# Which of three waits the last VectorE instruction carries itself

## The chip, the cores and the metric

One core of a Trainium2 chip. The metric is the device time of one execution in microseconds. Every run gives several; medians are quoted with the range. A profiled execution's span runs from its first to its last instruction and is some 1.4 us shorter than its time.

## The reference

The input `x` is 32 x 512 rows of 1024 floats, 67.1 MB. The output is the mean of `max(x, 0)` over each row.

```python
relu_x = np.maximum(x, 0)
return np.mean(relu_x, axis=-1).astype(np.float32)
```

## The kernel before

Each of 128 partitions holds 128 rows. Blocks of 16 rows are loaded into three buffers; ScalarE (ACT) sums the even rows, VectorE (DVE) the odd ones. The last row of each partition is cut into three loads so that little is left to do when the last bytes arrive. ScalarE sums columns 0-447, VectorE 448-575 and 576-767, each into a spare column behind the row. The last VectorE instruction sums columns 768-1023 and the three spare columns in one pass, scaled by 1/1024. It needs three things: the third load, VectorE's own two partial sums, and ScalarE's.

```python
    col_pieces = [576, 192, 256]
    # ... (loads, all issued by SyncE; loaded[k] counts to 16 when load k is complete)
    nc.scalar.wait_ge(loaded[i + 1], 16)
    act_row(nc, last[:, :448], last[:, D:D + 1]).then_inc(act, 1)
    nc.vector.wait_ge(loaded[i + 1], 16)
    dve_row(nc, last[:, 448:576], last[:, D + 1:D + 2])
    nc.vector.wait_ge(loaded[i + 2], 16)
    dve_row(nc, last[:, 576:768], last[:, D + 2:D + 3]).then_inc(dve, 1)
    nc.vector.wait_ge(dve, n_done + 1)          # VectorE's own sums
    nc.vector.wait_ge(loaded[i + 3], 16)        # the third load
    nc.vector.wait_ge(act, n_done + 1)          # ScalarE's sum
    nc.vector.scalar_tensor_tensor(
        out=last[:, 768:], in0=last[:, 768:], scalar=0.0, in1=scale[:, :], op0=ALU.max, op1=ALU.mult,
        accum_out=res[:, J - 1:J],
    ).then_inc(dve, 1)
    # ... SyncE waits for dve and stores the results
```

In the built program an engine's instruction carries one wait. Of several written in a row, the one written first is carried; the others go into a separate instruction (EVENT_SEMAPHORE) ahead of it, in reversed order. Here the separate instruction holds ScalarE's sum first and the load second, and the last instruction carries VectorE's own sum.

Of the kernel before, what the change touches and what calls it, by code (L numbers as in the profile page):

```python
# [17 lines left out]
def dve_row(nc, src, acc, init=None):  # L18

    return nc.vector.tensor_scalar(  # L20
        out=src, in0=src, scalar1=0.0, scalar2=init,
        op0=ALU.max, op1=ALU.add, accum_out=acc,
    )
# [22 lines left out]
def kernel(  # L46
# [10 lines left out]
    nc = tc.nc  # L57
# [36 lines left out]
    act, dve, pool = (nc.alloc_semaphore(n) for n in ("act", "dve", "pool"))  # L94
# [78 lines left out]
    for n in row_pieces[:-1]:  # L173
# [10 lines left out]
    n_done = i + 1  # L184
# [8 lines left out]
    dve_row(nc, last[:, 448:576], last[:, D + 1:D + 2])  # L193
    nc.vector.wait_ge(loaded[i + 2], 16)
    dve_row(nc, last[:, 576:768], last[:, D + 2:D + 3]).then_inc(dve, 1)
    nc.vector.wait_ge(dve, n_done + 1)
    nc.vector.wait_ge(loaded[i + 3], 16)
    nc.vector.wait_ge(act, n_done + 1)  # L198
    nc.vector.scalar_tensor_tensor(  # L199
        out=last[:, 768:], in0=last[:, 768:], scalar=0.0, in1=scale[:, :], op0=ALU.max, op1=ALU.mult,  # L200
        accum_out=res[:, J - 1:J],
# [51 lines left out]
```

## Time and profile before

| | before |
|---|---|
| time, 3 runs | 161.41 us (161.35 to 161.50) |
| span of the profiled execution | 159.8 us |

The page, the chain and the timeline of this stretch, and the moments at which the three conditions came true, are shown within the prediction; ScalarE's sum is the last of the three. Such a moment is the increment of a semaphore. It is read from the trace's records, to the nanosecond; no view of the profile prints it.

### The profile page before, as it was taken

The page shows a single profiled execution, that of the slowest core. Times are in us where ns is not written, and L with a number is a line of the kernel's source. Part 1 is how long each engine was busy: PE and PEld are TensorE (multiplying, and loading weights), DVE is VectorE, ACT ScalarE, POOL GpSimd, SP SyncE. Part 2 cuts the span into 40 slices and gives each one's busy share as a digit, 9 for nine tenths or more (in the row PEclk, how much of TensorE's full clock was granted, in tenths as well). Part 3 has the DMA queues.
Part 4 walks back from the last instruction along what each step waited for, and adds up shares of the span by engine and source line. Part 5 has one row for each costly group of instructions (what it writes and reads, how often), then busy time and mean ns, then how long its engine had stood idle before and what let it go on. Part 6 is the DMA issues. An engine that isn't in the chain of part 4 may idle for free.

```text
span 159.8 us, 350 instructions
## 1 busy us (share of the span) xinstructions
DVE 73.5 (46%) x133; ACT 70.4 (44%) x133; POOL 1.3 (1%) x9
## 2 busy tenths in 40 slices
DVE  0000029900498005970079500894009920199975
ACT  1400029800497005950079300892009900199974
POOL 1000000000000000000000000000000000000001
DMA  9969979999799699699699699799997997999993
GB/s 394 492 295 525 459 328 525 394 394 525 344 443 525 279 509 525 262 525 525 262 525 509 279 525 459 328 525 394 394 525 344 443 525 344 410 423 393 418 411 110
DMA packets 2456, 67.18 MB, mean 420 GB/s; under 512 B 536, under 2 KB 792, under 8 KB 1176
## 3 DMA queue, kind: packets, MB, share of 16 engines
q1 hardware_dynamic: 2456, 67.18, 97.9%
HBM read 67.11 MB, written 0.07 MB: 420 GB/s over the span
## 4 chain that ended last, share of the span: by engine, by line
DMA 84%; DVE 12%; SPq 1%; issue 1%; ACT 0%; DVEq 0%
DMA rows<-in_x_dram 56%; DMA last<-in_x_dram 29%; DVE rows L20 12%; SPq L109 1%; ACT last L15 0%; DVE last L199 0%; DVEq L198 0%; SPq L115 0%
## 5 line engine op out<-in xcount | busy, mean ns | idle before, releaser
L20 DVE TENSOR_SCALAR_CACHE_REDUCE rows<-rows 128x1024 f32<-128x1024 f32 (+1 forms) x63 | 72.1, 1208 | 78.8 <-DMA rows<-in_x_dram 78.7
L15 ACT ACTIVATE rows<-rows 128x1024 f32<-128x1024 f32 x64 | 66.3, 1038 | 84.0 <-DMA rows<-in_x_dram 83.7
L15 ACT ACTIVATION_READ_ACCUMULATOR rows<-rows 128x1 f32 x64 | 12.1, 189 | 0.0
L20 DVE DVE_READ_ACCUMULATOR rows<-rows 128x1 f32 x63 | 5.2, 83 | 0.0
L168 DVE STREAM_TRANSPOSE turned<-mean 128x32 f32<-128x32 f32 x1 | 0.2, 211 | 5.8 <-ACT row L164 5.8
L164 ACT ACT_TABLE_LOAD x1 | 1.3, 1283 | 3.2 <-DMA row<-in_x_dram 3.2
L157 POOL TENSOR_SCALAR res<-sums 128x112 f32<-128x112 f32 (+1 forms) x2 | 0.5, 250 | 153.8 <-DVE rows L20 153.8
L164 ACT ACTIVATE row<-row 128x1024 f32<-128x1024 f32 x1 | 1.1, 1057 | 0.0
L20 DVE TENSOR_SCALAR_CACHE_REDUCE last<-last 128x128 f32<-128x128 f32 (+1 forms) x2 | 0.6, 320 | 0.0
L15 ACT ACTIVATE last<-last 128x448 f32<-128x448 f32 x1 | 0.6, 577 | 0.1
L199 DVE SCALAR_TENSOR_TENSOR last<-last,scale 128x259 f32<-128x259 f32 x1 | 0.4, 429 | 0.2 <-ACT last L15 0.2
L142 POOL MEMSET scale<- 128x259 f32 x1 | 0.3, 315 | 0.0
L187 POOL TENSOR_SCALAR res<-part 128x1 f32<-128x1 f32 x1 | 0.3, 267 | 0.6 <-DVE rows L20 0.6
L15 ACT ACTIVATION_READ_ACCUMULATOR last<-last 128x1 f32 x1 | 0.2, 188 | 0.0
L164 ACT ACTIVATION_READ_ACCUMULATOR row<-row 128x1 f32 x1 | 0.2, 187 | 0.0
L20 DVE DVE_READ_ACCUMULATOR last<-last 128x1 f32 x2 | 0.2, 83 | 0.0
L141 POOL MEMSET mean<- 128x32 f32 x1 | 0.1, 125 | 1.5 <-POOLq L55 1.5
L237 POOL MEMSET const-bfloat16-1.0<- 128x1 bf16 x1 | 0.1, 102 | 0.0
L237 POOL MEMSET const-uint8-127<- 128x1 uint8 x1 | 0.1, 102 | 0.0
L237 POOL MEMSET const-float32-0.0<- 128x1 f32 x1 | 0.1, 99 | 0.2 <-issue 0.2
L237 POOL MEMSET const-float32-1.0<- 128x1 f32 x1 | 0.1, 99 | 0.0
L199 DVE DVE_READ_ACCUMULATOR last<-last,scale 128x1 f32 x1 | 0.1, 84 | 0.0
## 6 DMA issues: line engine op xcount, KB each, us to landing
rows<-in_x_dram SPq DMA_DIRECT2D x1, 3584.0 KB, 38.0
rows<-in_x_dram SPq DMA_DIRECT2D x1, 2048.0 KB, 42.5
rows<-in_x_dram SPq DMA_DIRECT2D x1, 1024.0 KB, 44.5
row<-in_x_dram SPq DMA_DIRECT2D x1, 512.0 KB, 3.2
rows<-in_x_dram SPq DMA_DIRECT2D x1, 512.0 KB, 45.3
last<-in_x_dram SPq DMA_DIRECT2D x1, 288.0 KB, 45.6
last<-in_x_dram SPq DMA_DIRECT2D x1, 128.0 KB, 45.2
rows<-in_x_dram SPq DMA_DIRECT2D x7, 48.7
```

The source lines that it names most:

```text
L15: return nc.scalar.activation(out=src, in_=src, func=ACT.Relu, accum_out=acc)
L20: return nc.vector.tensor_scalar(out=src, in0=src, scalar1=0.0, scalar2=init, op0=ALU.max, op1=ALU.add, accum_out=acc,)
L109: nc.sync.dma_start(out=dst, in_=src).then_inc(loaded[i], 16)
L141: nc.gpsimd.memset(mean0[:, :], 0.0)
L142: nc.gpsimd.memset(scale[:, :], inv).then_inc(pool, 1)
L157: nc.gpsimd.tensor_scalar(out=res[:, lo:hi], in0=sums[:, lo:hi], scalar1=inv, scalar2=0.0, op0=ALU.mult, op1=ALU.add,).then_inc(pool, 1)
L164: nc.scalar.activation(out=row0[:, :], in_=row0[:, :], func=ACT.Relu, scale=inv, accum_out=mean0[:, 0:1],).then_inc(first, 1)
L168: nc.vector.transpose(turned0[:, :], mean0[:, :]).then_inc(first, 1)
L187: nc.gpsimd.tensor_scalar(out=res[:, J - 2:J - 1], in0=part[:, 0:1], scalar1=part[:, 1:2], scalar2=inv, op0=ALU.add, op1=ALU.mult,).then_i ...
L199: nc.vector.scalar_tensor_tensor(out=last[:, 768:], in0=last[:, 768:], scalar=0.0, in1=scale[:, :], op0=ALU.max, op1=ALU.mult, accum_out=r ...
L237: nc = _bacc.Bacc("TRN2", target_bir_lowering=False, num_devices=1)
```

## The change

The order in which three waits are written. The intent: the instruction that is held for the last bytes should wait for them itself, and not through a separate instruction in front of it.

```diff
-    nc.vector.wait_ge(dve, n_done + 1)
     nc.vector.wait_ge(loaded[i + 3], 16)
     nc.vector.wait_ge(act, n_done + 1)
+    nc.vector.wait_ge(dve, n_done + 1)
     nc.vector.scalar_tensor_tensor(
```

In the built program the separate instruction now holds VectorE's own sum first and ScalarE's second, and the last instruction carries the load.

## The prediction

> **What bounds the kernel now.** I read the page from the top. The copies are the work: 67.11 MB are read at a mean of 420 GB/s in a span of 159.8 us, while VectorE and ScalarE are busy for less than half of it. The page's first two parts and its chain say so:
>
> ```profile
> span 159.8 us, 350 instructions
> DVE 73.5 (46%) x133; ACT 70.4 (44%) x133; POOL 1.3 (1%) x9
> ...
> HBM read 67.11 MB, written 0.07 MB: 420 GB/s over the span
> ...
> DMA 84%; DVE 12%; SPq 1%; issue 1%; ACT 0%; DVEq 0%
> ```
>
> What to see: the last entry, VectorE's sequencer (DVEq), has a share that rounds to nothing. The change touches that entry alone, so everything before the last few hundred nanoseconds can be left out. Next I read the end of the chain in order of time (start, length, what, in us):
>
> ```profile
> 111.47 45.58 DMA last<-in_x_dram
> 157.05 0.02 issue
> 157.07 0.06 ACT last L15
> 157.13 0.42 issue
> 157.55 0.20 ACT last L15
> 157.75 0.03 issue
> 157.78 0.05 DVEq L198
> 157.83 0.04 issue
> 157.87 0.12 DVE last L199
> ```
>
> This is the list that decides the case. The last row comes in three loads (columns 0-575, 576-767, 768-1023). The chain leaves the first of them at 157.05, runs through ScalarE's sum of columns 0-447, and reaches the last VectorE instruction through a waiting instruction of 0.05 us. It does not pass through the third load, the one this change is about. The timeline of the same stretch shows the VectorE side and the store (start, length, engine, line, operation, and in brackets the idle time before it):
>
> ```profile
> 157.07 0.58 ACT L15 ACTIVATE last<-last 128x448 f32<-128x448 f32 x1
> 157.34 0.35 DVE L20 TENSOR_SCALAR_CACHE_REDUCE last<-last 128x192 f32<-128x192 f32 x1
> 157.55 0.19 ACT L15 ACTIVATION_READ_ACCUMULATOR last<-last 128x1 f32 x1
> 157.62 0.08 DVE L20 DVE_READ_ACCUMULATOR last<-last 128x1 f32 x1
> 157.87 0.43 DVE L199 SCALAR_TENSOR_TENSOR last<-last,scale 128x259 f32<-128x259 f32 x1 [0.17 <-ACT last L15]
> 158.34 0.34 SPq L210 DMA_DIRECT2D out_dram<-res  x1
> ```
>
> The last VectorE instruction waits for three things, and the order in which they came true is the whole question. From the trace's record of semaphore increments, to the nanosecond: the third load's sixteenth increment is at 157.645, VectorE's own partial sum at 157.711, ScalarE's partial sum at 157.749. The load is first by 0.104 us and ScalarE is last, which is what the bracket above names.
>
> **What the Trainium skill says.** (1) "Perfetto Trace Analysis", section "DVE / Act Engine Instruction (TENSOR_ADD, Activation, etc)": such an instruction is pushed into a wait queue, its semaphores are met there, and it then moves on to the engine, while the sequencer is free for the next one. So a wait carried by the instruction should end in a start with little between. The trace agrees: the first load of the last row counts full at 157.047, and both engines start on it at 157.070 and 157.071, 0.023 to 0.024 us later. (2) The same page, "Identifying Dependency Chains": an instruction that waits for several engines may get EventSemaphore instructions ahead of it for the additional conditions. The trace shows one, on line 198, from 157.776 to 157.826, and the engine's instruction starts at 157.871. A condition met there thus costs 157.871 - 157.749 = 0.122 us from increment to start, against 0.024 us for a carried one: 0.098 us more. That difference is what moving a wait between the two places can be worth. (3) "VectorE: DVE Perf Modes", section "The DRAIN you can't avoid": a result read by the next instruction of the same engine is not safe without a semaphore between. The last instruction reads VectorE's two partial sums, so its wait on its own engine has to stay somewhere; the change keeps it, in the other place. No trace here tests that danger.
>
> **The change part by part.** In the built programs both kernels have the same instructions in the same order on every engine. The three waits are distributed differently. Before: the separate instruction holds (ScalarE's sum, third load), and the last VectorE instruction carries the wait for VectorE's own sum. After: the separate instruction holds (VectorE's own sum, ScalarE's sum), and the last VectorE instruction carries the third load. So:
>
> - Added: nothing. Removed: no instruction and no wait. The separate instruction still has two conditions, so I keep its 0.050 us.
> - Before, the separate instruction ends its wait at max(157.749, 157.645) = 157.749. After, at max(157.711, 157.749) = 157.749. Difference 0.000 us.
> - The carried wait is for 157.711 before and 157.645 after. Both precede the end of the separate instruction, 157.826, by over 0.11 us, so neither holds anything. Difference 0.000 us.
> - Behind it everything is as before: 0.43 us for the instruction, then the store of 7.5 KB. SyncE is released 157.871 + 0.465 = 158.336, and its last wait ends at 159.795, 1.46 us later. (4) The skill's "DMA: Bandwidth & Descriptors", section on where the fixed cost of about 2 us goes, puts most of that cost into the receipt of the written data; 1.46 us here for a tiny transfer fits in kind, and the change does not touch it.
> - The loads are all issued by 112.881 by SyncE, and no later issue waits on anything moved here, so the copies are untouched.
>
> Sum in the profiled execution: 0.000 us. The removal of the load from the separate instruction pays only in executions in which the load is the last of the three. With a lateness d beyond ScalarE's sum, before starts at load + 0.122, after at the later of load + 0.024 and ScalarE's sum + 0.122; so the gain is the smaller of d and 0.098 us. For d to be above zero the third load has to land more than 0.702 us after the first (157.749 - 157.047), against 0.598 us in the profile. The two loads between them are 96 KB + 128 KB, so their rate would have to fall by some 15%. I estimate that perhaps one execution in six does that, with a gain of some 0.05 us each: 0.01 us on the mean. That frequency is my choice; a single profile cannot give it.
>
> **The rivals.** *The load is often last without the profiler.* The intent of the change suggests that its author saw it so. For it: the slack is only 0.104 us, and the profiled execution (161.16 us) was 0.25 us shorter than the median of the others (161.41), so the copies may well fall differently. Against it: both the load and ScalarE's work start from the same stream, so a delay of all of it moves both. If every execution were so, the gain is at most 0.098 us: 161.31 us, still within 0.1%. *The order of the two conditions inside the separate instruction matters.* Its 0.050 us are against 0.021 us for VectorE's other separate waits, which hold one condition. If they are checked one after the other at some 0.029 us each, before pays the second check after ScalarE's sum has arrived, while after has the first check behind it by then: up to 0.029 us gained, 161.38 us. Against it: the record starts only at 157.776, 0.027 us after ScalarE's increment, so it may be a fixed execution time that comes after both conditions. I give this one chance in three. *The change takes something away.* With the load carried, a late load and a late sum could add up if the queue checked the load only after the separate instruction and needed longer for a load's semaphore than for the engine's own. Nothing in the profile speaks for that: 0.024 us is what carried loads show. It would make at most a few hundredths, 161.45 us. *ScalarE's sum stops being the last*, so that VectorE's own sum, at 157.711, binds: not possible by this change, which moves no work.
>
> **Range and chances.** 161.41 less 0.01 for the late loads and 0.01 (0.029 by one third) for the order of the checks makes 161.39 us. All mechanisms together span 161.28 (both gains in full) to 161.45. The three runs before lie within 0.15 us of each other, and a new set of runs may sit a tenth or two off for reasons of the copies alone, since the 67 MB are 84% of the chain and 0.1% of their rate is 0.13 us. I take 161.2 to 161.62. Two per cent would be 3.2 us, over thirty times the largest effect that I can build, so nearly all the chance is on "within 2%".
>
> **What would show it right or wrong.** In the profile of the changed kernel: equal instruction counts; the separate instruction, now on the line of the VectorE wait, still about 0.05 us long and still released by ScalarE's accumulator read; the last VectorE instruction some 0.12 us after ScalarE's increment, with the idle time before it near 0.17 us. If that distance is nearer 0.09 us, the order of the checks matters. If the load's last increment comes after ScalarE's, the instruction should start 0.024 us behind the load, and the first rival holds. I would be wrong if the time moved by over 0.3 us with the end of the trace unchanged, for then the copies moved, or if the separate instruction became longer or split in two.

## The result, and the profile after

The changed kernel took 161.16 us (median of 6 runs, 161.07 to 161.67) against 161.41 us (161.15 to 161.62, 6 runs): ratio 0.9990, 95% interval 0.9974 to 1.0006. A ratio is the mean time of one kernel's fast runs over that of the other's of the same rounds, so it is not quite the ratio of the medians. No difference is clear of noise.

The page of the changed kernel answers the first one line by line:

```profile
span 160.0 us, 350 instructions
DVE 73.5 (46%) x133; ACT 70.3 (44%) x133; POOL 1.3 (1%) x9
...
HBM read 67.11 MB, written 0.07 MB: 420 GB/s over the span
...
DMA 84%; DVE 12%; SPq 1%; issue 1%; ACT 0%; DVEq 0%
```

Same counts, same rate, same chain. This one execution has a span 0.2 us longer, because its copies came later: the first load of the last row is complete at 157.29 us instead of 157.05. So times from the span's start must not be compared across the two; distances from that load may be. The chain in order of time (start, length, what):

```profile
157.29 0.02 issue
157.31 0.06 ACT last L15
157.37 0.42 issue
157.79 0.20 ACT last L15
157.99 0.04 DVEq L198
158.03 0.04 issue
158.08 0.12 DVE last L199
```

Between ScalarE's accumulator read and the separate instruction (DVEq) stood a piece "issue" (time in which the engine waited for nothing that the profile shows) of 0.03 us; it is gone. From the first load to the last VectorE instruction it is 0.788 us here and 0.824 us before, so the end comes 0.036 us sooner. The timeline shows the idle time before the last instruction, which was marked 0.17 us; it is no longer marked, because it fell to 0.134 us and the timeline leaves out idle time under 0.15:

```profile
157.58 0.35 DVE L20 TENSOR_SCALAR_CACHE_REDUCE last<-last 128x192 f32<-128x192 f32 x1
157.79 0.19 ACT L15 ACTIVATION_READ_ACCUMULATOR last<-last 128x1 f32 x1
157.86 0.08 DVE L20 DVE_READ_ACCUMULATOR last<-last 128x1 f32 x1
158.08 0.43 DVE L199 SCALAR_TENSOR_TENSOR last<-last,scale 128x259 f32<-128x259 f32 x1
```

The semaphore records say why. VectorE's own sum is counted at 157.955, the separate instruction starts at 157.983, and ScalarE's sum is counted at 157.990. The separate instruction has started before its second condition is met. In the kernel before, it started 0.027 us behind ScalarE's increment; here, 0.028 us behind VectorE's own. The profile's start of such an instruction follows its first condition. The load (157.878) was early again and held nothing.

### The profile page after: what moved, and what is told of

It is laid out like the page before. It is cut to its first block, busy times and chain, and to the rows that moved or that the text cites. A ratio compares the mean times of both kernels' runs of the same rounds, so it can differ in the third digit from the quotient of the medians.

```text
span 160.0 us, 350 instructions
## 1 busy us (share of the span) xinstructions
DVE 73.5 (46%) x133; ACT 70.3 (44%) x133; POOL 1.3 (1%) x9
## 4 chain that ended last, share of the span: by engine, by line
DMA 84%; DVE 12%; SPq 1%; issue 1%; ACT 0%; DVEq 0%
DMA rows<-in_x_dram 56%; DMA last<-in_x_dram 29%; DVE rows L20 12%; SPq L109 1%; ACT last L15 0%; DVE last L199 0%; DVEq L198 0%; SPq L115 0%
## 5 line engine op out<-in xcount | busy, mean ns | idle before, releaser
L15 ACT ACTIVATE rows<-rows 128x1024 f32<-128x1024 f32 x64 | 66.2, 1036 | 84.0 <-DMA rows<-in_x_dram 83.8
```

The costliest lines, as they stand in the source:

```text
L15: return nc.scalar.activation(out=src, in_=src, func=ACT.Relu, accum_out=acc)
```

## The experiments

Two theories at the outset. **S (serial)**: the separate instruction checks its conditions one after the other, so the place of a wait in it matters. **R (removal)**: what matters is that the load left the separate instruction. For the 0.25 us in the medians there are two more: **C**, that the change affects the copies, and **N**, that it is noise. Distances are between semaphore increments and starts, from the traces. All twelve runs gave correct results. Four variants ran only once (161.09, 161.29, 161.25 and 162.03 us, in the order of this section); only distances within their traces are read.

### The changed kernel once more

No edit.

> The changed kernel once more, timed in five rounds, because the first comparison left 0.25 us (161.16 against 161.41), seven times the 0.034 us that the ends of the two traces differ by. Theory S (the separate instruction checks its two conditions one after the other; the profile's start of it is the moment when the first is met): the last VectorE instruction starts at the later of first condition + 0.122 us and second condition + at most 0.088 us, so here about 0.088 us behind ScalarE's increment, and the time is 0.03 us below before: ratio 0.9998. Rival C (the copies became faster by the change): ratio again near 0.9985.

161.16 us (161.07 to 161.47) against 161.42 us; ratio 0.9988, 0.9974 to 1.0003. In this profile the load is the last of the three: it is counted 0.728 us behind the first load, ScalarE's sum 0.700, VectorE's own 0.663. The last instruction starts at 0.785, which is VectorE's own + 0.122 and ScalarE's + 0.085. So even with the load last, the load held nothing: a carried wait would have let the instruction start at some 0.751. C and N stay open.

### The order within the separate instruction

```diff
     nc.vector.wait_ge(loaded[i + 3], 16)
-    nc.vector.wait_ge(act, n_done + 1)
     nc.vector.wait_ge(dve, n_done + 1)
+    nc.vector.wait_ge(act, n_done + 1)
```

> The changed kernel with the two conditions of the separate instruction swapped: ScalarE's sum first, VectorE's own second; the load stays carried by the last instruction. Theory S: ScalarE's sum is now the first to be checked and the last to come, so the last instruction starts 0.122 us behind its increment, as in before. Rival R (what matters is that the load left the separate instruction): 0.088 us, as in the changed kernel.

The chain of this variant:

```profile
157.49 0.20 ACT last L15
157.69 0.03 issue
157.71 0.05 DVEq L198
157.76 0.04 issue
157.81 0.12 DVE last L199
```

The piece "issue" of 0.03 us ahead of the separate instruction is back, and the last instruction starts 0.122 us behind ScalarE's increment, as in the kernel before, although the load is carried. So R is wrong: taking the load out of the separate instruction gained nothing here, and the 0.036 us are due to the order.

### The load first in the kernel before

```diff
     nc.vector.wait_ge(dve, n_done + 1)
-    nc.vector.wait_ge(loaded[i + 3], 16)
     nc.vector.wait_ge(act, n_done + 1)
+    nc.vector.wait_ge(loaded[i + 3], 16)
```

> The kernel before with the two conditions of the separate instruction swapped: the load first, ScalarE's sum second; the instruction still carries the wait for VectorE's own sum. Theory S: at most 0.088 us from ScalarE's increment to the start, although the load is still in the separate instruction; the separate instruction's record starts 0.027 us behind the load's last increment, before ScalarE's. Rival R: 0.122 us, as in before.

This run missed its aim. In the profiled execution the load was the last by 0.170 us, so ScalarE's sum did not bind and the 0.088 us could not be seen:

```profile
157.86 0.03 issue
157.89 0.05 DVEq L198
157.94 0.04 issue
157.99 0.12 DVE last L199
```

What it does show: the separate instruction starts 0.028 us behind the load, now its first condition, and the last instruction 0.123 us behind it. The cost of the first place is the same for a load's semaphore as for an engine's.

### Carrying the wait that comes last

```diff
-    nc.vector.wait_ge(dve, n_done + 1)
-    nc.vector.wait_ge(loaded[i + 3], 16)
     nc.vector.wait_ge(act, n_done + 1)
+    nc.vector.wait_ge(dve, n_done + 1)
+    nc.vector.wait_ge(loaded[i + 3], 16)
```

> The last instruction carries the wait for ScalarE's sum, which comes last; the separate instruction holds the load first and VectorE's own sum second. Theory S: start at the latest of load + 0.122, own sum + at most 0.088, ScalarE's sum + 0.024: with the spacings of before (load 0.104, own sum 0.038 ahead of ScalarE's) at most 0.050 us behind ScalarE's increment, so some 0.07 us earlier than before; ratio about 0.9996, which five rounds may not resolve. Rival R: the load is in the separate instruction, so 0.122 us.

The chain goes straight from ScalarE to the last instruction, and the separate instruction (its own entry, durations in ns) is longer, since it starts at the load and waits inside for VectorE's own sum:

```profile
157.50 0.20 ACT last L15
157.69 0.04 issue
157.73 0.12 DVE last L199
```

```profile
L198 DVEq EVENT_SEMAPHORE  x1: 102/102/102, 157.6 to 157.6; - x1
```

The start is 0.041 us behind ScalarE's increment and 0.080 us behind VectorE's own, so VectorE's own sum, as the second condition, now sets it. From the first load it is 0.741 us: 0.083 less than in the kernel before, 0.047 less than in the changed one. The time was 161.33 us (161.02 to 161.47), ratio 0.9997, 0.9983 to 1.0011: a gain of this size isn't seen in the time. R is refuted once more, with the load in the separate instruction.

### The same with VectorE's own sum first

```diff
     nc.vector.wait_ge(act, n_done + 1)
-    nc.vector.wait_ge(dve, n_done + 1)
     nc.vector.wait_ge(loaded[i + 3], 16)
+    nc.vector.wait_ge(dve, n_done + 1)
```

> As the variant that carries ScalarE's sum, with the separate instruction's conditions swapped: VectorE's own sum first, the load second. Theory S: start 0.122 us behind VectorE's own increment, so about 0.085 us behind ScalarE's (own sum 0.038 us ahead in before), 0.035 us later than with the load first. If the order did not matter, as with the load first.

The start is 0.122 us behind VectorE's own increment and 0.086 us behind ScalarE's, 0.786 us from the first load: as S had it, 0.045 us later than with the load first.

### A load that comes last on purpose

All three of these have this edit (and a `scale` buffer of 643 columns in place of 259), with the waits of before, of the changed kernel, and with the load first in the separate instruction:

```diff
-    col_pieces = [576, 192, 256]
+    col_pieces = [320, 64, 640]
-    act_row(nc, last[:, :448], last[:, D:D + 1]).then_inc(act, 1)
+    act_row(nc, last[:, :192], last[:, D:D + 1]).then_inc(act, 1)
-    dve_row(nc, last[:, 448:576], ...); dve_row(nc, last[:, 576:768], ...); the rest: last[:, 768:]
+    dve_row(nc, last[:, 192:320], ...); dve_row(nc, last[:, 320:384], ...); the rest: last[:, 384:]
```

> The case that the change is meant for, made on purpose: the last row's loads are 320, 64 and 640 columns wide and ScalarE sums 192 of them, VectorE 128 and 64, so that the third load comes last by some 0.3 us (both partial sums some 0.5 us behind the first load, the third load 352 KB at 420 GB/s = 0.84 us behind it). Waits as in before: the separate instruction has ScalarE's sum, then the load; the instruction carries VectorE's own. Theory S: the load is the second condition, the first long met, so the last instruction starts at most 0.088 us behind the load's last increment, and the separate instruction's record is stretched: it starts 0.027 us behind ScalarE's increment. Without serial checks: 0.122 us behind the load.

> The same late load with the waits of the changed kernel: the instruction carries the load. Start 0.024 us behind the load's last increment, 0.06 us (theory S) to 0.10 us (no serial checks) sooner after the load than with the waits of before. The time falls by as much, under 0.1%, which three rounds may not resolve.

> The same late load, the separate instruction holding the load first and ScalarE's sum second. Theory S: the late one is the first condition, so 0.122 us behind the load's last increment, 0.034 us or more later than with the load second. If only the place of a wait counts and not its order: the same distance as with the load second.

The chains, with the waits of before (first the separate instruction's own entry), then of the changed kernel, then with the load first:

```profile
L198 DVEq EVENT_SEMAPHORE  x1: 389/389/389, 157.4 to 157.4; - x1
```

```profile
112.48 45.26 DMA last<-in_x_dram
157.74 0.04 DVEq L198
157.78 0.04 issue
157.82 0.12 DVE last L199
```

```profile
112.58 45.21 DMA last<-in_x_dram
157.79 0.02 issue
157.81 0.07 DVE last L199
```

```profile
112.49 45.59 DMA last<-in_x_dram
158.07 0.03 issue
158.10 0.05 DVEq L198
158.15 0.04 issue
158.20 0.12 DVE last L199
```

In the first the separate instruction is recorded as running for 389 ns: it starts 0.027 us behind ScalarE's increment and 0.354 us before the load's. From the load's last increment to the last instruction it is 0.079 us with the load second, 0.023 us with the load carried, and 0.122 us with the load first. All three sizes of S are thereby measured on the same, clearly last condition. (The 352 KB of the first expectation are the second and the third load together.) In the time, the first two are 161.51 and 161.50 us, with ratios to before of 1.0017 (0.9994 to 1.0040) and 1.0011 (0.9988 to 1.0034): 0.056 us between them can't be resolved. The third, a single run of 162.03 us, had its third load 1.338 us behind the first, against 0.957 and 0.923; its time is not compared.

### Is there more in the time than in the trace?

A null run of the kernel before against itself, and again the changed kernel and the variant that carries ScalarE's sum, on the same rounds; then the changed kernel a fourth time.

> The kernel before, unchanged, timed against itself: how far apart two identical kernels come out in five rounds. If by 0.1% (0.16 us), then the 0.0010 to 0.0012 by which the changed kernel lay below in two comparisons needs no cause in the change (theory N, noise of the copies). If within 0.0003, the 0.15 to 0.25 us wants a cause beyond the 0.034 us at the end of the trace (theory C).

> The changed kernel on the same rounds. Theory N: ratio anywhere from 0.9985 to 1.001, and about as far from 1 as the null run. Theory C: 0.9988 a third time, with the null run at 1.000. In its profile the last VectorE instruction starts 0.122 us behind VectorE's own increment, unless ScalarE's comes over 0.043 us later than that or the load over 0.099 us later.

> The variant that carries ScalarE's sum on the same rounds: its trace ended 0.04 us sooner than the changed kernel's after the first load of the last row. Theory N: ratio within 0.0015 of 1, its order against the changed kernel left to chance. In its profile the start is 0.080 us behind VectorE's own increment, or 0.122 us behind the load's if that is later than 0.042 us before VectorE's own.

> The changed kernel a fourth time against before. So far 0.9990, 0.9988 and 0.9993, each with 1 in its interval, and the null run at 1.0010; the ends of the traces give 0.9998 (0.037 us), or 0.9997 (at most 0.056 us) when the third load is late. Theory N: the fourth ratio lies anywhere between 0.9985 and 1.0010. Theory C (a part of the gain that the end of the trace doesn't show): again 0.9985 to 0.9995. In its profile, the start is the latest of own sum + 0.122, ScalarE's sum + 0.080 and load + 0.023.

| kernel, against before | median us | ratio | 95% interval |
|---|---|---|---|
| before itself | 161.35 against 161.19 | 1.0010 | 0.9991 to 1.0030 |
| changed | 161.14 against 161.19 | 0.9993 | 0.9978 to 1.0007 |
| carrying ScalarE's sum | 161.09 against 161.19 | 0.9993 | 0.9978 to 1.0008 |
| changed, fourth time | 161.15 against 161.17 | 0.9992 | 0.9976 to 1.0008 |

Two identical kernels came out 0.1% apart, as far as the changed one from before. Yet four ratios of the changed kernel, 0.9990, 0.9988, 0.9993 and 0.9992, all lie below 1. I therefore looked at all runs together, after the fact: 52 of the kernel before have a mean of 161.34 us, 24 of the changed one 161.20. Most of this 0.13 us comes from executions above 161.3 us, 23 of 52 and 4 of 24. The runs below it have means of 161.15 and 161.13 us, 0.02 apart, which is near what the trace shows. The variant that carries ScalarE's sum, with a shorter end than both, had 5 of 12 above 161.3 us. That speaks against a link between the waits and the slower executions, but the cut was chosen after the fact.

Taken as independent comparisons, the four ratios average 0.9991, give or take 0.0008 (an estimate from their intervals). That lies below 1, and just holds the 0.9998 that the ends of the traces lead to expect. So a gain beyond the traces is neither shown nor excluded. The profiles show where slower executions lose their time. In the two of the kernel before, timed at 161.16 and 161.19 us, the first load of the last row is complete at 157.05 and 157.08 us. In the four of the changed kernel, timed at 161.11, 161.23, 161.36 and 161.70 us, it is complete at 157.04, 157.08, 157.29 and 157.64 us. From there to the end of the timed execution it is 4.06 to 4.15 us in all six. So nearly all of the difference between executions arises in the copies, ahead of the waits that were changed, and the copies of the changed kernel are at most 0.004 us earlier than those of before. That is no sign of C, but six profiles do not decide it: C against N stays open.

## Why the prediction was right or wrong

All traces follow one formula. The last instruction starts at the latest of: first condition of the separate instruction + 0.122 us, second condition + 0.080 us, carried condition + 0.023 us. The first number was taken from the trace of before, the second from the first run that carries ScalarE's sum, the third from the late load with the waits of the changed kernel. In the other eleven profiles the first number sets the start in eight and the second in three; the third sets it in none of them, so it is measured once, for a load. (For ScalarE's sum, the second profile that carries it shows a start 0.028 us behind its increment, so the delay is no longer than that.) In ns from the last increment of the first load:

| profile (first, second; carried) | load | own | ScalarE | formula | measured |
|---|---|---|---|---|---|
| before (ScalarE, load; own) | 598 | 664 | 702 | 824 | 824 |
| before, null run (the same) | 554 | 646 | 700 | 822 | 823 |
| changed (own, ScalarE; load) | 588 | 665 | 700 | 787 | 788 |
| changed, second profile | 728 | 663 | 700 | 785 | 785 |
| changed, third | 727 | 659 | 700 | 781 | 782 |
| changed, fourth | 593 | 654 | 701 | 781 | 782 |
| (ScalarE, own; load) | 592 | 680 | 701 | 823 | 823 |
| (load, ScalarE; own) | 870 | 696 | 700 | 992 | 993 |
| (load, own; ScalarE) | 566 | 661 | 700 | 741 | 741 |
| (load, own; ScalarE), second | 554 | 649 | 701 | 729 | 729 |
| (own, load; ScalarE) | 585 | 664 | 700 | 786 | 786 |
| late load (ScalarE, load; own) | 957 | 671 | 576 | 1037 | 1036 |
| late load (own, ScalarE; load) | 923 | 680 | 583 | 946 | 946 |
| late load (load, ScalarE; own) | 1338 | 685 | 588 | 1460 | 1460 |

The records of the separate instruction show what the first two numbers are made of. It starts 0.027 to 0.029 us behind its first condition. It ends 0.050 us later (0.054 once), or 0.035 to 0.036 us behind its second condition if that is later. Where it sets the start, the last instruction follows 0.044 to 0.045 us behind its end. So 0.122 = 0.027 + 0.050 + 0.045, and 0.080 = 0.035 + 0.045. That the two conditions are checked one after the other is the reading that fits all this; what the traces show is the delays.

- **The time, 161.39 us in 161.2 to 161.62, within 2%.** Measured 161.16 us in the first comparison. That is just outside the low end of the range, by 0.04 us, while the four medians of the changed kernel lie between 161.14 and 161.16; so in absolute time the range was a little too high. Applied to the time that the prediction started from, the measured ratio gives 0.9990 x 161.41 = 161.25 us, which is inside. That the change stays within 2% was right, but it was no test of the mechanism: every rival of the prediction would have stayed within it too. (The effects were over thirty times smaller than 2% only one at a time; both gains together, 0.127 us, are 25 times smaller.) The range was laid around the 161.41 us of three runs of before; its 52 runs have a median of 161.22, so the centre was high by some 0.2 us.
- **"Difference 0.000 us" for the separate instruction: wrong.** This is the step that failed. It took the end of its wait as the maximum of two conditions. The conditions are not alike: each has its own delay to the start. The sum should have been 824 - 787 = 37 ns; measured 36, and 39 to 42 in the other three profiles of the changed kernel against the first of before. The sign that the prediction named for this came: the last instruction starts 0.088 us behind ScalarE's increment, "nearer 0.09" than 0.12, and the idle time before it is 0.134 us and not 0.17.
- **The order of the two checks, one chance in three and 0.029 us: right in kind.** It is what happens, and the second place costs 0.042 us less than the first, not 0.029. The argument against it, that the record starts only behind ScalarE's increment, misread the record: in before, ScalarE's was simply the first condition.
- **"Not possible by this change" that VectorE's own sum binds: wrong.** In three of the four profiles of the changed kernel it is what sets the start (own + 0.122 against ScalarE's + 0.080), in one of them by only 0.001 us. No work moved, but the weights of the waits did.
- **The gain for a late load, "the smaller of d and 0.098 us": mis-sized.** With the waits of before the load is second, 0.080 and not 0.122, so carrying it is worth at most 0.057 us (0.056 measured: 0.079 less 0.023), and nothing until the load is 0.042 us behind ScalarE's sum. In the two profiles of the changed kernel with the load last by 0.027 to 0.028 us, it did not count: the start came 0.055 and 0.057 us behind the load, not 0.024. The size for a carried load itself was right: 0.023 us with the late load.
- **One execution in six with the load last.** In eleven profiles with the original pieces it was last in three. It is not rare, but the change's stated intent still did not set the start in any profile of the changed kernel.
- **Copies untouched, same instructions, the end otherwise as before: right.** From the last VectorE instruction to the end of the span it is 1.941 us before and 1.936 us after. That stretch varies by itself, though: from 1.935 to 2.018 us in the eleven profiles with the original pieces, the longest in the second profile of the changed kernel. This spread is twice the gain.

## What to carry to other kernels

When an instruction waits for several things, let it carry the one that comes last, and put the one that comes earliest first in the separate instruction ahead of it; here that arrangement shortened the way from the first load to the last instruction by 0.083 and 0.095 us in its two profiles, where the change that was asked about gained about 0.04. This was tried on one instruction of VectorE alone. Do not take the latest condition alone as the bound: add to each the delay of its place and then take the latest. Before timing such a change, compare its largest possible gain (here under 0.1 us of 161) with a null run of the same kernel (here 0.16 us apart in the medians), and read it from distances in the trace instead.

## What the Trainium skill lacked or had wrong

- "Perfetto Trace Analysis", section "Identifying Dependency Chains", says that additional conditions may go into EventSemaphore instructions, but not what they cost or that their order counts: 0.122 us from increment to start for the first condition, 0.080 us for the second, 0.023 us for the carried one.
- The same page, section "Sequencer-only Instruction (DRAIN, etc)", gives the profiler's start as the moment when all semaphores are satisfied. For a VectorE EVENT_SEMAPHORE with two conditions it follows the first one by 0.027 to 0.029 us: with the late load and the waits of before it was recorded for 389 ns and began 0.354 us before its second condition was met.
- "DMA: Bandwidth & Descriptors", section "Anatomy of one DMA — SWDGE (gpsimd) path", fits a fixed cost of about 2.0 us for copies issued by GpSimd, and the page has no such fit for a store issued by SyncE. The 7.5 KB store issued by SyncE here took 1.46 us from issue to the end of the last wait before, 1.45 us after, and 1.54 us in the second profile of the changed kernel.
